# Where a narrow expert's up columns are summed, and which rows a gather fetches: one change to a two-block mixture-of-experts kernel

## The chip, the cores and the metric

The kernel runs on one core of one Trainium2 chip. The metric is the device time of one execution in microseconds (us); three executions of the kernel before are shown, with their median. The profile is a fourth execution, recorded by the hardware profiler.

The engines are called as the profile calls them: PE (TensorE, matrix products), PEld (its weight loads), DVE (VectorE), ACT (ScalarE), POOL (GpSimd), SP (SyncE, which here only issues transfers). Transfers run on 16 DMA engines that all queues share: q1 holds what SP issues, q0 what POOL issues.

## The reference

A transformer block with a short convolution and an expert-choice feed-forward is followed by a second block: an mLSTM and pooling mixer, then a hierarchical mixture of 32 experts. The change touches only the second mixture. Cut to what matters:

```
def hierarchical_moe(h, w_rg, b_rg, w_re, b_re, w_gate, w_up, w_down):
    g_idx = argmax(hf @ w_rg + b_rg)             # one of 4 groups for each of 1024 tokens
    top_val, top_loc = lax.top_k(e_logits, 2)    # 2 of the group's 8 experts
    ...
    def run_block(args):
        a = xb @ w_gate[e]                       # 1024 -> 512
        b = xb @ w_up[e]                         # 1024 -> 512
        return (silu(a) * b) @ w_down[e]         # 512 -> 1024
    out = out * slot_gate[:, None]
    y = zeros((n_tok, dm)).at[slot_tok].add(out)
```

There are 1024 tokens with 2 experts each, 2048 assignments in all. Each expert's three weight matrices are 2 MB each in float32, and all of them are loaded once.

## The kernel before

**Slots.** The 32 experts are put into 32 slots, in an order that depends on how many tokens chose them. A slot has a fixed number of places: 256 (two blocks of 128) in slots 5, 10, 15 and 20 (`PAIRS_AT`), 128 in slots 0 to 2 and in nine more, 64 in slots 26 to 31 (`HALF_AT`), 32 in ten slots (`QUARTER_AT`: 6, 7, 11, 12, 16, 17, 21, 22, 25, 24). Two narrow slots of 32 follow each pair slot, and two more follow slot 23. A place without a token has `src` 0 and `idx` above 8000: `src` names token 0, while `idx` is outside the table, and an indirect transfer skips it (`bounds_check`). The places are 20 x 128 + 6 x 64 + 10 x 32 = 3264.

Counted from the reference's router on the inputs, these are the tokens by slot:

| slots | places each | tokens |
|---|---|---|
| 0, 1, 2 | 128 | 5, 11, 3 |
| 5, 10, 15, 20 | 256 | 158, 169, 213, 162 |
| 3, 4, 8, 9, 13, 14, 18, 19, 23 | 128 | 124, 111, 71, 77, 115, 116, 124, 108, 116 |
| 6, 7, 11, 12, 16, 17, 21, 22, 24, 25 | 32 | 20, 7, 3, 13, 31, 7, 2, 4, 0, 8 |
| 26 to 31 | 64 | 49, 49, 37, 34, 54, 47 |

**Order of work.** `unit_order` writes the program: for slot i, gate (`g`) and up (`u`) products, then the transposes `xT` of slot i+1, then the down product (`d`) of slot i-1, then the transposes `hT` of slot i. So in the program, slot 7's up columns stand ahead of slot 6's down product, and both behind the pair slot 5's down product.

**Weights.** `Loader` issues chunks of 1 MB from SP in exactly that order into 14 buffers (`raw`), with at most four in flight (`N_FLIGHT`). A wide slot's chunk is split in two parts into high and low float32r halves (ACT line 191, DVE line 192, tile `hl`, 5 buffers, `N_SPLIT`), and PE makes three products of them (lines 199 to 201). A narrow slot (32 or 64 places) uses the chunk unsplit (line 556). A buffer is free when its split, or its products, are done.

**Narrow slots of 32 places.** The products leave partial sums in four bands of 32 rows of one PSUM bank. `few_sums` copies two bands to the tile `whole` (ACT line 567; one buffer) and adds the other two to them (DVE line 570): first the gate columns into `hid`, then the up columns into `up`, a piece of an output tile `yo`. ACT applies silu, and DVE line 676 multiplies. The down product's two halves are summed in the same way, into the `yo` that is then scattered.

**Output tiles.** `yo` has two buffers in turn. Each output (DVE line 741 for wide slots, 690/691 for narrow ones) takes one, and POOL scatters it with accumulation into `acc_d` (line 518); the buffer is free when the scatter has landed. Scatters into `acc_d` also wait for each other. The up columns of a narrow slot take a `yo` too, so in the stretch that the prediction reads, the turns are: slot 4's output, slot 6's up, slot 5's two outputs, slot 7's up, slot 6's output, slot 7's output.

**Gathers.** POOL gathers a block's rows of `h_d` (4 KB each) into `xg` (line 512, two buffers) by `src`, at the place where the block before the one before has been transposed. 36 gathers serve the 32 slots.

Of the kernel before, what the change touches and what calls it, by code (L numbers as in the profile page):

```python
# [18 lines left out]
OP = mybir.AluOpType  # L19
# [4 lines left out]
D = 1024  # L24
# [98 lines left out]
def kernel(ctx, tc, a, out):  # L123
    nc = tc.nc
# [7 lines left out]
    def sub_pool(stack, name, bufs=1, side=None):  # L132
        return stack.enter_context(tc.tile_pool(name=name, bufs=bufs, reuse_waits="tile", side=side))
# [8 lines left out]
    def mm_ps(kind="mm"):  # L142
        return banks[kind].tile([P, 2, 512], F32, tag=kind, name=kind)

    def aux_ps(n=512, kind="aux"):
        return banks[kind].tile([P, n], F32, tag=kind, name=kind)
# [33 lines left out]
    acc_d = [dram.tile([T, D], F32, name=f"acc{b}_d") for b in range(2)]  # L180
    h_d = [dram.tile([T, D], F32, name=f"h{b}_d") for b in range(2)]
    mod_d = dram.tile([12, D], F32, name="mod_d")
# [168 lines left out]
    def proj_T(hl, hT, n=P):  # L351

        ps = mm_ps()
        for half in range(2):
            proj_half(ps[:, half], hl, hT, half, n)
        return ps
# [140 lines left out]
    class Experts:  # L497
# [60 lines left out]
        def few_sums(self, ps, m, outs):  # L558

            if m == P // 2:  # L560
                for i, o in enumerate(outs):
                    if o is not None:
                        nc.scalar.copy(o, ps[i * m:(i + 1) * m])
                return
            t = self.tile("whole", [512], 1)
            for at in (P // 2, 0):
                nc.scalar.copy(t[at:at + m], ps[at + m:at + 2 * m])
            for i in (1, 0):
                at = i * (P // 2)
                nc.vector.tensor_tensor(outs[i], ps[at:at + m], t[at:at + m], op=OP.add)  # L570

        def product(self, sT, hl, ps, ks, last):
            for i, k in enumerate(ks):
# [2 lines left out]
    def chunks(e, wg, wu, wd, fdim):  # L576

        b = {}
        for kind, w, kdim, n in (("g", wg, D, fdim), ("u", wu, D, fdim), ("d", wd, fdim, D)):
            m = kdim * n // (P * 2048)  # L580
            b[kind] = [(("x", e, kind, c), w, c, m, n) for c in range(m)]
        return b

    def run_experts(hlp, blocks, route):
# [9 lines left out]
        def ahead(lo=nc.vector):  # L594
            if todo and (todo[0][1] or ld.is_ready(todo[0][0])):
                key, part = todo.popleft()
                if part == 0:
                    raws[key] = ld.take(key)
                raw = raws[key]
                raw = raw[:, part].rearrange("p (h f) -> p h f", h=2) if raw.shape[2] == D else raw[:, part * KP:(part + 1) * KP]  # L600
                hl = hlp.tile([P, 2, KP, 512], F32R, tag="hl", name="hl")
                split(hl, raw, lo)
                if part == N_PARTS - 1:
                    ld.done(key)
                hls.append(hl)
# [19 lines left out]
        ex, late = route(meanwhile)  # L625
        fd = ex.fdim
        subs = deque(s for b in blocks for s in b["subs"])
# [10 lines left out]
        ps, gate_raw = None, None  # L638

        def few(i, kind, c):  # L640

            nonlocal ps, gate_raw
            s = blocks[i]["subs"][0]
            m = s["m"]
            key, _, ci, n_ch, _ = c
            raw = ld.take(key)
            if key[2] == "g":
                gate_raw = key, raw
                if ci == 0:
                    ps = mm_ps()[:, 0]  # L650
                return
            if kind == "u":
                for b in range(4):
                    ex.product_few(s["xT"], (raw[:, b], gate_raw[1][:, b]), ps, ci * 4 + b, 7)
                ld.done(gate_raw[0])
            else:
                if ci == 0:
                    ps = mm_ps()[:, 0]
                for b in range(2):
                    ex.product_few(s["hT"], [raw[:, b, h * 512:(h + 1) * 512] for h in range(2)], ps, ci * 2 + b, 3)  # L660
            ld.done(key)
            for _ in range(N_PARTS):
                if len(hls) < N_SPLIT:
                    ahead()
            if ci < n_ch - 1:
                return
            if kind == "u":
                s["hid"] = hid = ex.tile("hid", [fd], ex.wide)[:m]
                if m == P // 2:
                    nc.scalar.activation(hid, ps[m:], AF.Silu)  # L670
                    nc.vector.tensor_tensor(hid, ps[:m], hid, op=OP.mult)
                else:
                    up = ex.tile("yo", [D], ex.wide)[:m, 0:fd]
                    ex.few_sums(ps, m, (up, hid))
                    nc.scalar.activation(hid, hid, AF.Silu)
                    nc.vector.tensor_tensor(hid, up, hid, op=OP.mult)
                return
            if "keep" in s:
                upper = ex.tile("whole", [512], 1)[:m]
                ex.few_sums(ps, m, (None, upper))  # L680
                s["keep"](ps[:m], s, 0)
                s["keep"](upper, s, 1)
                return
            y = ex.tile("yo", [D], ex.wide)
            if m == P // 2:
                ex.few_sums(ps, m, (None, y[:m, 512:]))
                nc.vector.scalar_tensor_tensor(y[:m, :512], ps[:m], s["gate"][:m], ex.grow[:m, :512], op0=OP.mult, op1=OP.mult)
                nc.vector.scalar_tensor_tensor(y[:m, 512:], y[:m, 512:], s["gate"][:m], ex.grow[:m, 512:], op0=OP.mult, op1=OP.mult)
            else:
                ex.few_sums(ps, m, (y[:m, :512], y[:m, 512:]))  # L690
                nc.vector.scalar_tensor_tensor(y[:m], y[:m], s["gate"][:m], ex.grow[:m], op0=OP.mult, op1=OP.mult)
            ex.scatter(y, s["idx"], m)
            if "after" in s:
                s["after"]()

        for n_unit, (i, kind, c) in enumerate(units):
# [10 lines left out]
            if blocks[i].get("small"):  # L707
                few(i, kind, c)
                continue
            _, _, ci, n_ch, width = c  # L710
            kgs = (fd if kind == "d" else D) // P
            if ci == 0:

                if width == D:
                    ps = [mm_ps() for _ in bl]
                else:
                    two = mm_ps()
                    ps = [two[:, j:j + 1] for j in range(len(bl))]
# [427 lines left out]
    def block2(x_src):  # L1146
# [65 lines left out]
        for h in range(4):  # L1212
            ps = pss[h] if h < 3 else proj_T(ft.next(), hT)
# [9 lines left out]
        with ExitStack() as s3:  # L1223
# [6 lines left out]
            ps = proj_T(wifs, hT, 8)  # L1230
# [3 lines left out]
            for tt in range(NT):  # L1234
                ps = mm_ps()
# [16 lines left out]
        with ExitStack() as s3:  # L1252
# [40 lines left out]
            for slot in range(2 * NT):  # L1293
# [5 lines left out]
                ps = aux_ps(kind="half")  # L1299
# [39 lines left out]
        def ready_tile(tt):  # L1339
# [6 lines left out]
            if tt == NT - 1:  # L1346
# [4 lines left out]
        blocks = [chunks(s, *[w[N_EXP2 - N_FIRST + s] if s < N_FIRST else ("dyn", w, s) for w in ws], 512)  # L1351
                  for s in range(N_EXP2)]
# [18 lines left out]
        with ExitStack() as s3:  # L1371
# [3 lines left out]
            def route2(meanwhile):  # L1375
                sl = s3.enter_context(ExitStack())
                r = route_groups(sub_pool(sl, "rtl2", side="right"), sub_pool(s0, "rt2"), L, meanwhile)
                slot_row[0] = r["row"]
                s0.close()
                for s, b in enumerate(blocks):  # L1380
                    cols = [s] + ([N_EXP2 + PAIRS_AT.index(s)] if s in PAIRS_AT else [])
                    b["subs"] = [dict(src=r["src"][:, c:c + 1], idx=r["idx"][:, c:c + 1], gate=r["gate"][:, c:c + 1]) for c in cols]
                    if b["small"]:
                        b["subs"][0]["m"] = SMALL[s]
                blocks[-1]["subs"][0]["keep"] = keep_rows
                blocks[-2]["subs"][-1]["after"] = load_sums
                ex = Experts(None, sub_pool(s3, "xg2"), h_d[1], acc_d[1], mod_d[11:12, :], 512, 2, wide=2)
                lists.append((r, ex))

                def late():  # L1390
                    yield from r["late"]()
                    yield
                    sl.close()
                    ex.pool = sub_pool(s3, "xp2")
                    ex.row()
                return ex, late()
# [29 lines left out]
            def keep_rows(ps, s, h):  # L1426
# [5 lines left out]
                nc.vector.tensor_tensor(rows[m:, c], y, rows[:m, c].bitcast(F32), op=OP.subtract)  # L1432

            run_experts(hlp, blocks, route2)
            r, ex = lists[0]
            ld.drop_pools()
# [580 lines left out]
```

## Time and profile before

| | |
|---|---|
| median of 3 runs | 2093.81 us (2092.6 to 2098.33) |
| profiled execution, own time | 2095.92 us |
| its span in the trace | 2094.0 us |
| PE, PEld, DVE, ACT, POOL busy | 91%, 71%, 72%, 49%, 16% of the span |
| transfers | 573.56 MB, mean 274 GB/s |

The span is what the trace covers; the time is 1.92 us more. The second mixture fills the span from about 1480 to 2062 us. Busy shares are means over stages with different limits, so the rows below are read by stretch. A DMA share of about 1.02 is what the windows show when the 16 engines are full.

### The profile page before, as it was taken

The page shows a single profiled execution, that of the slowest core. Times are in us where ns is not written, and L with a number is a line of the kernel's source. Part 1 is how long each engine was busy: PE and PEld are TensorE (multiplying, and loading weights), DVE is VectorE, ACT ScalarE, POOL GpSimd, SP SyncE. Part 2 cuts the span into 40 slices and gives each one's busy share as a digit, 9 for nine tenths or more (in the row PEclk, how much of TensorE's full clock was granted, in tenths as well). Part 3 has the DMA queues.
Part 4 walks back from the last instruction along what each step waited for, and adds up shares of the span by engine and source line. Part 5 has one row for each costly group of instructions (what it writes and reads, how often), then busy time and mean ns, then how long its engine had stood idle before and what let it go on. Part 6 is the DMA issues. An engine that isn't in the chain of part 4 may idle for free.

```text
span 2094.0 us, 25405 instructions
## 1 busy us (share of the span) xinstructions
PE 1903.0 (91%) x9192; PEld 1494.4 (71%) x9192; DVE 1502.5 (72%) x1934; ACT 1036.3 (49%) x1454; POOL 332.4 (16%) x300
## 2 busy tenths in 40 slices
PE   4999999949999999999789999898799898898986
PEld 3788888837888888888667787686687576676432
DVE  6699985567999999999744357666896767575414
ACT  4311123216787878787654244332575546464313
POOL 1045430032010110000100000101411211111210
PEclk7999999969999999999989999999899999999998
DMA  9467746288999999999422001426798989999998
GB/s 322 139 231 261 255 160 223 111 295 310 388 384 403 386 402 388 401 381 373 111 97 80 16 31 36 163 111 248 312 387 293 401 325 382 350 391 338 369 386 317
DMA packets 154108, 573.56 MB, mean 274 GB/s; under 512 B 30311, under 2 KB 53575, under 8 KB 104828
## 3 DMA queue, kind: packets, MB, share of 16 engines
q1 hardware_dynamic: 134812, 511.78, 63.5%
q0 software_dynamic: 18784, 59.46, 9.9%
q8 instruction: 73, 1.20, 0.2%
q10 hardware_dynamic: 384, 0.68, 0.1%
q14 instruction: 55, 0.45, 0.1%
HBM read 534.12 MB, written 42.66 MB: 275 GB/s over the span
## 4 chain that ended last, share of the span: by engine, by line
PE 64%; DMA 13%; issue 11%; DVE 7%; ACT 2%; POOL 2%; DVEq 0%; POOLq 0%; SPq 0%; ACTq 0%
PE mm L201 17%; PE mm L199 17%; PE mm L200 17%; DMA raw<-in_w_expert_up_dram 4%; DMA acc_d<-yo,idx 4%; DMA raw<-in_w_expert_down_dram 2%; PE aux L533 2%; PE half L201 1%; PE half L199 1%; PE half L200 1%; PE aux L417 1%; PE aux L1595 1%; POOL acc_d L518 1%; DVE hl L192 1%; POOL xg L512 1%
## 5 line engine op out<-in xcount | busy, mean ns | idle before, releaser
L192 DVE TENSOR_TENSOR hl<-raw,hl 128x1024 fp32r<-128x1024 f32 x601 | 718.2, 1232 | 141.1 <-ACT hl L191 123.1
L191 ACT CAST hl<-raw 128x1024 fp32r<-128x1024 f32 x612 | 634.9, 1054 | 266.6 <-PE mm L201 233.9
L199 PE MATMUL mm<-hl,xT 128*128 128x512 f32 x832 | 331.1, 398 | 0.2 <-ACT xT L195 0.2
L200 PE MATMUL mm<-hl,xT 128*128 128x512 f32 x832 | 327.7, 394 | 0.0
L201 PE MATMUL mm<-hl,xT 128*128 128x512 f32 x832 | 327.7, 394 | 0.0
L199 PE MATMUL mm<-hT,hl 128*128 128x512 f32 x448 | 179.3, 400 | 8.2 <-ACT hT L879 5.9
L199 PEld LDWEIGHTS mm<-hl,xT 128*128 128x128 f32 x832 | 159.1, 191 | 33.2 <-ACT xT L195 0.7
L201 PEld LDWEIGHTS mm<-hl,xT 128*128 128x128 f32 x832 | 158.3, 190 | 34.1 <-issue 0.4
L200 PEld LDWEIGHTS mm<-hl,xT 128*128 128x128 f32 x832 | 158.7, 191 | 32.3
L200 PE MATMUL mm<-hT,hl 128*128 128x512 f32 x448 | 177.0, 395 | 0.2 <-DVE hT L880 0.2
L201 PE MATMUL mm<-hT,hl 128*128 128x512 f32 x448 | 176.6, 394 | 0.0
L199 PE MATMUL mm<-hl,hT 128*128 128x512 f32 x416 | 164.9, 396 | 0.2 <-ACT hT L195 0.2
L201 PE MATMUL mm<-hl,hT 128*128 128x512 f32 x416 | 162.6, 391 | 1.0 <-DVE hT L196 1.0
L200 PE MATMUL mm<-hl,hT 128*128 128x512 f32 x416 | 162.2, 390 | 0.0
L199 PEld LDWEIGHTS mm<-hT,hl 128*128 128x128 f32 x448 | 85.5, 191 | 26.7 <-ACT hT L879 6.4
L556 PE MATMUL mm<-raw,xT 128*32 128x512 f32 (+1 forms) x512 | 85.8, 621 | 16.3 <-DMA raw<-in_w_expert_up_dram 16.3
L301 DVE SCALAR_TENSOR_TENSOR adacc<-adaw,ccol,adacc 128x512 f32<-128x512 f32 x142 | 100.0, 771 | 0.0
L200 PEld LDWEIGHTS mm<-hT,hl 128*128 128x128 f32 x448 | 85.4, 191 | 18.9 <-DVE hT L880 1.4
L518 POOL DMA_INDIRECT acc_d<-yo,idx x35 | 54.0, 1543 | 280.3 <-DVE yo L741 123.9
L201 PEld LDWEIGHTS mm<-hT,hl 128*128 128x128 f32 x448 | 85.3, 190 | 18.1
L201 PEld LDWEIGHTS mm<-hl,hT 128*128 128x128 f32 x416 | 78.1, 188 | 17.9 <-DVE hT L196 1.4
L199 PEld LDWEIGHTS mm<-hl,hT 128*128 128x128 f32 x416 | 78.4, 188 | 16.1 <-ACT hT L195 0.4
(485 smaller groups left out, 2971.7 us busy)
## 6 DMA issues: line engine op xcount, KB each, us to landing
raw<-in_moe_w_gate_dram SPq DMA_DIRECT2D x64, 1024.0 KB
raw<-in_moe_w_up_dram SPq DMA_DIRECT2D x64, 1024.0 KB
raw<-in_moe_w_down_dram SPq DMA_DIRECT2D x64, 1024.0 KB
raw<-in_w_expert_gate_dram SPq DMA_DIRECT2D x64, 1024.0 KB
raw<-in_w_expert_down_dram SPq DMA_DIRECT2D x63, 1024.0 KB
raw<-in_w_expert_up_dram SPq DMA_DIRECT2D x62, 1024.0 KB
adaw<-in_ada_w_dram SPq DMA_DIRECT2D x47, 1024.0 KB
raw<-in_sc_w_in_dram SPq DMA_DIRECT2D x9, 1024.0 KB
```

Source lines behind the costliest of these rows:

```text
L191: nc.scalar.copy(hl[:, 0], raw)
L192: lo.tensor_tensor(hl[:, 1], raw, hl[:, 0].bitcast(F32), op=OP.subtract)
L199: nc.tensor.matmul(o, s_hi, m_hi, start=start, stop=False)
L200: nc.tensor.matmul(o, s_hi, m_lo, start=False, stop=False)
L201: nc.tensor.matmul(o, s_lo, m_hi, start=False, stop=stop)
L301: nc.vector.scalar_tensor_tensor(acc[kk % 2], w[:, k], c, add, op0=OP.mult, op1=OP.add)
L417: nc.tensor.matmul(o, xT[:, k], rsc[:, k], start=k == 0, stop=k == KC - 1)
L512: nc.gpsimd.indirect_dma_start(out=x[:m], out_offset=None, in_=self.src, in_offset=bass.IndirectOffsetOnAxis(ap=idx[:m], axis=0), bounds_c ...
L518: nc.gpsimd.indirect_dma_start(out=self.acc, out_offset=bass.IndirectOffsetOnAxis(ap=idx[:m], axis=0), in_=y[:m], in_offset=None, compute_ ...
L533: nc.tensor.transpose(ps[:, i * P:(i + 1) * P], self.block(x, k, tag), ident)
L556: nc.tensor.matmul(ps[at:at + m], sT[:, k], w, start=k < split, stop=k > last - split)
L1595: nc.tensor.matmul(ps[:, h * P:(h + 1) * P], a_, b_, start=True, stop=True)
```

## The change

Two edits, both in the second mixture.

`few_sums` may now be given `None` for an output, and then sums into the rows of `whole` that hold the copied band, and returns them. A slot of 32 places uses that for its up columns, which no longer take a turn of `yo`.

The gathers of all blocks but the first two use `idx` instead of `src`, so a place without a token is skipped and its row of `xg` keeps what was there. The first two fill both buffers of `xg` with finite rows (`ex_n_x`, 2, is the number of these buffers). A skipped row's result is never scattered.

```
                 at = i * (P // 2)
-                nc.vector.tensor_tensor(outs[i], ps[at:at + m], t[at:at + m], op=OP.add)
+                nc.vector.tensor_tensor(t[at:at + m] if outs[i] is None else outs[i], ps[at:at + m], t[at:at + m], op=OP.add)
+            return t[:m]
...
-                    up = ex.tile("yo", [D], ex.wide)[:m, 0:fd]
-                    ex.few_sums(ps, m, (up, hid))
+                    up = ex.few_sums(ps, m, (None, hid))
                     nc.scalar.activation(hid, hid, AF.Silu)
                     nc.vector.tensor_tensor(hid, up, hid, op=OP.mult)
...
                 r = route_groups(sub_pool(sl, "rtl2", side="right"), sub_pool(s0, "rt2"), L, meanwhile)
                 slot_row[0] = r["row"]
+                ex_n_x = 2
                 s0.close()
...
+                for sub in [sub for b in blocks for sub in b["subs"]][ex_n_x:]:
+                    sub["src"] = sub["idx"]
                 blocks[-1]["subs"][0]["keep"] = keep_rows
                 blocks[-2]["subs"][-1]["after"] = load_sums
-                ex = Experts(None, sub_pool(s3, "xg2"), h_d[1], acc_d[1], mod_d[11:12, :], 512, 2, wide=2)
+                ex = Experts(None, sub_pool(s3, "xg2"), h_d[1], acc_d[1], mod_d[11:12, :], 512, ex_n_x, wide=2)
```

No engine gets or loses an instruction, and none changes its place; the targets and the waits change. On DVE, around slots 5 to 7 of the kernel before (the two L741 are slot 5's outputs, the first two L570 slot 7's gate and up columns, the next two slot 6's down columns; a wait on DMASW is one on a transfer that POOL issued, here a scatter):

```order
L741 SCALAR_TENSOR_TENSOR yo<-mm,gate_11080,grow 128x1024 [waits DMASW4_49,PE_49]
L741 SCALAR_TENSOR_TENSOR yo<-mm,gate_11080,grow 128x1024 [waits DVE_49,PE_49]
L192 TENSOR_TENSOR hl<-raw,hl 128x1024 [waits DMAHW3_49,Activation_49]
L570 TENSOR_TENSOR hid<-mm,whole 32x512 [waits PE_49,Activation_49]
L570 TENSOR_TENSOR yo<-mm,whole 32x512 [waits DMASW6_49,DVE_49]
L676 TENSOR_TENSOR hid<-yo,hid 32x512 [waits DVE_49,Activation_49]
L196 TENSOR_TENSOR xT<-aux,xT 128x512 [waits Activation_49] x2
L570 TENSOR_TENSOR yo<-mm,whole 32x512 [waits DVE_49,PE_49,Activation_49]
L570 TENSOR_TENSOR yo<-mm,whole 32x512
L691 SCALAR_TENSOR_TENSOR yo<-yo,gate_11080,grow 32x1024 [waits DVE_49]
L192 TENSOR_TENSOR hl<-raw,hl 128x1024 [waits Activation_49]
```

The up columns wait there for the scatter of semaphore 6, ahead of slot 8's `xT`. The same place on DVE in the changed kernel:

```order
L741 SCALAR_TENSOR_TENSOR yo<-mm,gate_11080,grow 128x1024 [waits DMASW2_49,PE_49]
L741 SCALAR_TENSOR_TENSOR yo<-mm,gate_11080,grow 128x1024 [waits DMASW4_49,PE_49]
L192 TENSOR_TENSOR hl<-raw,hl 128x1024 [waits DMAHW3_49,Activation_49]
L570 TENSOR_TENSOR hid<-mm,whole 32x512 [waits PE_49,Activation_49]
L570 TENSOR_TENSOR whole<-mm,whole 32x512 [waits DVE_49]
L676 TENSOR_TENSOR hid<-whole,hid 32x512 [waits DVE_49,Activation_49]
L196 TENSOR_TENSOR xT<-aux,xT 128x512 [waits Activation_49] x2
L570 TENSOR_TENSOR yo<-mm,whole 32x512 [waits DMASW6_49,PE_49,Activation_49]
L570 TENSOR_TENSOR yo<-mm,whole 32x512
L691 SCALAR_TENSOR_TENSOR yo<-yo,gate_11080,grow 32x1024 [waits DVE_49]
L192 TENSOR_TENSOR hl<-raw,hl 128x1024 [waits Activation_49]
```

The wait for semaphore 6 has moved three rows down, behind slot 8's `xT`, to slot 6's down columns. The four further pairs of narrow slots change alike. On POOL, as the difference of the two programs, at the third gather (`src` and `idx` are the index tables):

```order
 L92 DMA raw<-in_w_expert_down_dram 128x2048
 L192 TENSOR_TENSOR hl<-raw,hl 128x1024 x2
-L512 DMA xg<-h_d,src_11051 128x1024
+L512 DMA xg<-h_d,idx_11053 128x1024
 L504 DMA grow<-mod_d 128x1024
```

Only the index table of the gather differs; its place does not.

## Rows read from the trace of the kernel before

**Rows 1.** Windows: us; busy PE, PEld, DVE, ACT, POOL; PEclk; DMA share; GB/s
```profile
1640.00:1737.00 97.00, 89.20 (x457) 67.68 (x456) 66.64 (x69) 52.71 (x66) 16.32 (x12) 0.96 0.94 359
1737.00:1834.00 97.00, 88.35 (x457) 67.02 (x456) 66.53 (x68) 52.72 (x66) 15.31 (x12) 0.96 0.98 367
1834.00:1931.00 97.00, 89.88 (x459) 68.13 (x458) 67.11 (x70) 52.71 (x66) 15.34 (x12) 0.96 0.97 363
1931.00:2057.00 126.00, 108.91 (x542) 49.00 (x540) 33.61 (x40) 27.89 (x46) 18.51 (x15) 0.93 1.02 381
```

**Rows 2.** Windows of 10 us, same columns
```profile
1690.00:1700.00 10.00, 10.00 (x48) 8.19 (x47) 5.25 (x6) 3.93 (x5) 0.81 (x1) 1.00 0.53 197
1500.00:1510.00 10.00, 8.63 (x44) 7.20 (x43) 8.34 (x9) 7.03 (x9) 1.03 (x1) 1.00 1.02 418
1630.00:1640.00 10.00, 2.09 (x8) 1.74 (x9) 4.03 (x7) 1.73 (x4) 2.62 (x2) 0.67 1.02 390
```

**Rows 3.** SP's queue waits, 1490 to 2094: total us, times, longest
```profile
SPq L92 <- DVE hl L192: 164.9, 66, 6.0
```

**Rows 4.** Waits of the engines, 1490 to 2094, same columns
```profile
PE aux L541 <- DVE xT L196: 28.1, 4, 8.4
DVE yo L570 <- DMA acc_d<-yo,idx: 27.5, 5, 6.9
```

**Rows 5.** Timeline of DVE: start, us, operation, [idle before]
```profile
1627.87 0.68 DVE L570 TENSOR_TENSOR hid<-mm,whole 32x512 f32<-32x512 f32 x1 [2.30 <-ACT whole L567]
1635.44 0.68 DVE L570 TENSOR_TENSOR yo<-mm,whole 32x512 f32<-32x512 f32 x1 [6.88 <-DMA acc_d<-yo,idx]
...
1637.18 1.27 DVE L196 TENSOR_TENSOR xT<-aux,xT 128x512 fp32r<-128x512 f32 x2
1638.48 1.38 DVE L570 TENSOR_TENSOR yo<-mm,whole 32x512 f32<-32x512 f32 x2
1639.90 1.27 DVE L691 SCALAR_TENSOR_TENSOR yo<-yo,gate,grow 32x1024 f32<-32x1024 f32 x1
```

**Rows 6.** Timeline of ACT, the same stretch
```profile
1629.24 1.07 ACT L195 CAST xT<-aux 128x512 fp32r<-128x512 f32 x2
1641.48 1.04 ACT L191 CAST hl<-raw 128x1024 fp32r<-128x1024 f32 x1 [2.59 <-PE mm L201]
```

**Rows 7.** Timeline of PE, the same stretch
```profile
1637.91 0.68 PE L541 MATMUL aux<-ident,hid 32*128 32x32 f32 x4 [8.36 <-DVE xT L196]
1638.52 0.79 PE L199 MATMUL mm<-hl,xT 128*128 128x512 f32 x1
...
1641.24 0.63 PE L199 MATMUL mm<-hl,xT 128*128 128x512 f32 x1
1641.67 0.63 PE L200 MATMUL mm<-hl,xT 128*128 128x512 f32 x1
...
1644.44 0.39 PE L199 MATMUL mm<-hl,xT 128*128 128x512 f32 x1
1644.67 0.39 PE L200 MATMUL mm<-hl,xT 128*128 128x512 f32 x1
```

**Rows 8.** Chain that ended last, pieces: start, us, what
```profile
1623.53 11.82 DMA acc_d<-yo,idx
...
1636.11 9.67 DMA acc_d<-yo,idx
...
2046.75 10.98 DMA raw<-in_w_expert_down_dram
```

**Rows 9.** Queue q0 in 1602.5:1604.5 (gather of slot 8, 128): packets, MB, share
```profile
q0 software_dynamic: 144, 0.52, 65.5%
```

**Rows 10.** Queue q0 in 1628:1634.5 (scatter, 128)
```profile
q0 software_dynamic: 143, 0.52, 40.6%
```

**Rows 11.** Queue q0 in 1671.5:1673.5 (gather of slot 11, 32 places)
```profile
q0 software_dynamic: 45, 0.13, 21.9%
```

**Rows 12.** Queue q0 in 1748.5:1750 (scatter of slot 11)
```profile
q0 software_dynamic: 33, 0.01, 5.2%
```

## Prediction

> **What bounds the kernel now.** I read the windows first, because the change lies in one stage, the second mixture (1480 to 2062 us), and shares over the whole span mix it with others. From 1640 to 1931 us there are three equal cycles of 97 us. Each holds one pair slot, two narrow slots and two wide ones, 30 chunks of weights. PE is busy for 88 to 90 us of each, and the DMA engines at 0.94, 0.98 and 0.97 [rows 1]. From 1931 to 2057 us, where the half slots come, the DMA share is 1.02 [rows 1], which is what full looks like, and the chain that ended last is a string of weight loads up to the last one [rows 8]. So the end of the stage is set by transfers, and what decides the total is how much work the 16 engines have and how long they sit idle before the last chunk.
>
> Why are they ever idle? The 10 us around 1690 show it: PE busy all the time, DMA share 0.53 [rows 2]. That is the pair slot, where PE needs longest for a chunk; all 14 buffers are full, and SP waits for a split to free one (164.9 us in all) [rows 3]. There PE holds the transfers up, and time that PE loses earlier in the cycle comes back here as idle DMA time.
>
> PE does lose time: 28.1 us in four waits for DVE's `xT` [rows 4]. The timeline shows one. DVE sums slot 7's gate columns at 1627.87 us, then stands 6.88 us at the up columns, since these want the `yo` that slot 5's first output still occupies; its scatter takes 11.82 us from issue to landing [rows 5, 8]. Behind it wait slot 8's `xT`, and behind these PE, idle for 8.36 us [rows 5, 7]. The granted clock is then 0.67 in the mean of these 10 us [rows 2], and the next products come 0.43 us apart instead of 0.23 [rows 7].
>
> **The change part by part, the sums.** DVE does the same additions at the same place. The wait for the scatter moves from slot 7's up columns to slot 6's down columns, three rows further, behind slot 8's `xT`. It isn't removed: it can still last until about 1635.4 us. What is gained is what PE can do meanwhile.
>
> Step by step for this place. The up sum starts where the gate sum ends, 1628.55, and takes 0.68; the product with silu takes about as long, to 1629.95. ACT has the high halves of `xT` ready between 1629.8 and 1630.3 [rows 6]. The first low half takes about 0.68, so PE's transposes start at about 1630.7 instead of 1637.91, 7.2 us earlier [rows 5, 7]; PE's idle time falls from 8.36 to 1.15 us. Its products follow 0.61 later [rows 7], at 1631.3. Five split parts lie ready: ACT could cast a sixth only at 1641.48, when PE had given a buffer back [rows 6]. A part is six products, so at 0.227 us each they last 6.8 us, to 1638.1. DVE comes free from the scatter's landing at 1635.4, plus 1.38 for slot 6's sums, 1.27 for its output [rows 5] and 1.2 for the split, at 1639.3: PE waits 1.2 us. Before, the sixth part's turn came at 1638.52 plus 12 products at 0.43 and 18 at 0.227, or 1647.7 [rows 7]. So PE gains 8.4 us here. If its clock drops anyhow, the five parts last 2.4 us longer, which hides DVE's lateness, and the gain is 7.2.
>
> There are four such places [rows 4]: 28.1 less 4 x 1.15 is 23.5 us that PE starts earlier; with the clock kept, another 2.4 at most for each. PE's side could move by 23 to 31 us.
>
> The transfers cannot follow that far. Against a full 1.02, the cycles' shares leave (0.08 + 0.04 + 0.05) x 97 = 16.5 us of idle [rows 1]; the stretch from 1931 on leaves none.
>
> The second edit makes the transfers' work smaller. The trace shows what a skipped place costs, at the scatters, which already use `idx`: slot 11 has 32 places and 3 tokens; its gather moves 0.13 MB [rows 11], its scatter 0.01 MB, with 33 packets of which all but three are tiny [rows 12]. A gather of 128 full rows has 65.5% of 2.0 us, 1.31 us of all engines or 10.2 ns a row [rows 9]; one of 32 rows 0.44 us or 13.7 ns a row [rows 11]. (A scatter's row costs twice as much, 40.6% of 6.5 us for 128 [rows 10], and stays.) Of 3264 places 1216 are empty; slots 0 and 1 keep their 240, so 976 rows go. 338 of these are in slots 2 to 8, the last of them gathered at 1604 us [rows 9], while PE and full buffers still rule: they buy nothing. After that 638 go, 336 from gathers of 128 and 302 from narrow ones: 3.4 + 4.1 = 7.6 us, or 6.5 at the lower price throughout; I take 7. POOL still issues as many gathers. Bounds for the price of a skipped row: nothing, as at the scatters, or as much as a full row, if the reading is wrong; I take nothing, since it is the same instruction with the same table.
>
> Now both sides together. In the first cycle the transfers' idle time of 7.8 us, and some 1.8 saved by 160 rows, stand against PE's 7.2 to 8.4, so up to 2 us of idle stays. In the second, 3.9 + 1.0 against 5 to 8, and in the third, 4.9 + 2.1 against 6 to 9: none stays, and PE eats into the stock of full buffers, some ten chunks, without emptying it. So the transfers gain 16.5 + 7 - 2 = 21.5 us, and the four places of PE, with 23 to 31, do not bind. The end behind the last chunk (from 2057.7) stays. I take 21.
>
> The profiled time, 2095.92, is 2.1 us above the median, so it goes to 2075 and the median of 2093.81 to 2073, 1.0% less. A measurement here can tell about 0.3%, 6.3 us, from no change.
>
> **A rule against it.** The Trainium skill, DMA: Bandwidth & Descriptors, section Where 436 GB/s comes from, puts transfers between HBM and SBUF under a limit of about 358 GB/s for a core. By that the cycles, at 359 to 367 GB/s, would have nothing to regain. This case's trace doesn't agree: one 10 us window moves 418 GB/s [rows 2]. By the page's rule the change would be worth 7 us, by the rows 21.
>
> **Rivals.**
> 1. *Half the stall comes back.* The wait now stands ahead of the next splits, and slot 7's down columns need the `yo` of slot 5's second output, whose scatter lands 9.67 us after 1636.11, at 1645.8 [rows 8]; with PE 8 us earlier DVE wants it less than 2 us later. If PE keeps only a third to two thirds of its gain, the total is 8 to 17 us: 2077 to 2086.
> 2. *The transfers have no slack.* The windows' dips would then be bursts evened out, and only the 7 us of rows come off: 2087. SP's waits for a free buffer [rows 3] and the 418 GB/s speak against it.
> 3. *The wait only moves.* If PE stood still until DVE passes slot 6's sums, say because the five parts weren't ready, only the tail's 138 rows (24 in slot 25, 114 in the half slots) would count, at 13.7 ns: 1.9 us, 2092. The cast that waited for PE speaks against it [rows 6].
> 4. *More.* If transfers run at their best rate whenever buffers are free, PE's side binds: 25 to 31 us, 2063 to 2069.
> 5. *Slower.* The loads now never pause, so scatters queue behind more of them. From the landing DVE needs 3.9 us to PE's next part; PE is worse off than before once that landing comes after 1647.7 - 3.9 = 1643.8, that is 20.3 us after issue instead of 11.8. At 24 us four places lose 3.7 each: 15 less the tail's 2, 2107. Landings of 10 to 12 us in a stretch that was already full [rows 2, 8] speak against it.
>
> **How the numbers follow.** My forecast, 18 to 25 us off, gets 0.50; rival 1 0.24; rival 2 0.05; rival 3 0.09; rival 4 0.06; rival 5 0.06. The likeliest is 2073, its own range 2069 to 2076. With rivals 1, 2 and most of 4, 2064 to 2088 holds some 0.84. Faster by over 0.3% (below 2087.5): the forecast, rivals 1 and 4, and three fifths of 2, 0.83. Within 0.3%: the rest of 2 and rival 3, 0.11. Slower 0.06.
>
> **What would show it.** In the profile after: no wait of DVE for a scatter at the up columns; a wait of 3 to 6 us at slot 6's down columns and its like; PE's idle time at these places near 1 us, and the clock near 1.00 there; the dips of the DMA share in the pair slots after the first nearly gone; queue q0 smaller by about 4.0 MB (976 x 4096); the dip in slot 5, ahead of these places, unchanged; the stretch behind the last chunk unchanged. It would be wrong if the dips stay although PE no longer waits, or if DVE's new wait grows.

## The result, and the profile after

The changed kernel takes 2075.78 us in the median (2073.99 to 2078.27, 4 runs) against 2094.79 us (2092.6 to 2098.33, 4 runs) beside it: a ratio of 0.9905, with a 95% interval of 0.9893 to 0.9917. That is 19 us faster; 2073 was forecast. The profiled execution took 2075.67 us with a span of 2073.7, 20.3 us less than the span before.

**The place that was worked out.** This is the timeline of DVE in the changed kernel, at the stretch of [rows 5].

```profile
1628.05 0.69 DVE L570 TENSOR_TENSOR hid<-mm,whole 32x512 f32<-32x512 f32 x1 [2.25 <-ACT whole L567]
1628.76 0.68 DVE L570 TENSOR_TENSOR whole<-mm,whole 32x512 f32<-32x512 f32 x1
1629.55 0.68 DVE L676 TENSOR_TENSOR hid<-whole,hid 32x512 f32<-32x512 f32 x1
1630.16 1.27 DVE L196 TENSOR_TENSOR xT<-aux,xT 128x512 fp32r<-128x512 f32 x2
1634.96 1.38 DVE L570 TENSOR_TENSOR yo<-mm,whole 32x512 f32<-32x512 f32 x2 [3.54 <-DMA acc_d<-yo,idx]
1636.38 1.27 DVE L691 SCALAR_TENSOR_TENSOR yo<-yo,gate,grow 32x1024 f32<-32x1024 f32 x1
1637.58 8.02 DVE L192 TENSOR_TENSOR hl<-raw,hl 128x1024 fp32r<-128x1024 f32 x7
...
1648.55 1.38 DVE L570 TENSOR_TENSOR yo<-mm,whole 32x512 f32<-32x512 f32 x2
```

The up columns (second line) start right behind the gate columns. The wait for the scatter is there still, but behind slot 8's `xT` and for 3.54 us. The last line, slot 7's down columns, waits for nothing. And PE's timeline, to set beside [rows 7]:

```profile
1630.88 0.67 PE L541 MATMUL aux<-ident,hid 32*128 32x32 f32 x4 [1.12 <-DVE xT L196]
1631.48 0.50 PE L199 MATMUL mm<-hl,xT 128*128 128x512 f32 x1
...
1638.42 0.39 PE L199 MATMUL mm<-hl,xT 128*128 128x512 f32 x1
1638.84 0.50 PE L200 MATMUL mm<-hl,xT 128*128 128x512 f32 x1
1639.17 0.39 PE L201 MATMUL mm<-hl,xT 128*128 128x512 f32 x1
```

The sixth part's first product, before:

```profile
1647.84 0.39 PE L199 MATMUL mm<-hl,xT 128*128 128x512 f32 x1
```

And the 10 us of [rows 2] that had a granted clock of 0.67, in the changed kernel:

```profile
1630.00:1640.00 10.00, 9.09 (x40) 7.29 (x41) 6.41 (x9) 7.56 (x11) 4.08 (x2) 1.00 1.03 392
```

PE is idle for 1.12 us instead of 8.36, the products stay 0.23 us apart, and the granted clock is 1.00, the upper of its two levels (2.4 GHz). PE takes five split parts in a row. The sixth begins at 1638.42 with the product that reads the high half (line 199), and its second product, which reads the low half, comes after a pause of 0.2 us, at 1638.84.

**The stage.** Waits of the engines after (us in all, times, longest), to set beside [rows 4]:

```profile
DVE yo L570 <- DMA acc_d<-yo,idx: 12.2, 4, 3.5
PE aux L541 <- DVE xT L196: 4.5, 4, 1.1
```

SP's queue, to set beside [rows 3]:

```profile
SPq L92 <- DVE hl L192: 113.4, 45, 6.0
```

SP waits 51 us less for a split to free a buffer. Windows of the changed kernel, three stretches of 92 us and what follows (columns as in [rows 1]):

```profile
1640.00:1732.00 92.00, 88.29 (x464) 67.03 (x463) 67.98 (x70) 53.77 (x67) 28.72 (x13) 1.00 1.00 379
1732.00:1824.00 92.00, 88.74 (x464) 67.08 (x463) 67.24 (x70) 53.92 (x68) 28.41 (x13) 1.00 1.01 383
1824.00:1916.00 92.00, 88.30 (x469) 66.91 (x472) 68.05 (x71) 52.88 (x67) 24.56 (x13) 1.00 1.01 388
1916.00:2040.00 124.00, 101.20 (x502) 41.26 (x498) 25.86 (x34) 21.07 (x40) 18.93 (x15) 0.93 0.99 372
```

The clock is 1.00 instead of 0.96, and the DMA share is at its full 1.00 to 1.01. The last row includes 10 us in which the transfers run out (0.77 from 2030 to 2040). A stretch of 92 us is a little longer than a cycle of the engines. Measured from the output of slot 6 to those of slots 11, 16 and 21 (DVE line 691, at 1639.90, 1736.97, 1834.19 and 1930.76 us before and 1636.38, 1726.60, 1817.57 and 1907.47 after), the sums over three such windows are, before and after:

```profile
sum 290.86, PE 267.29 PEld 202.69 DVE 200.14 ACT 158.14 POOL 46.97; mean PE 89.10 PEld 67.56 DVE 66.71 ACT 52.71 POOL 15.66
sum 271.09, PE 260.38 PEld 196.73 DVE 198.62 ACT 157.60 POOL 80.92; mean PE 86.79 PEld 65.58 DVE 66.21 ACT 52.53 POOL 26.97
```

So a cycle of the engines is 90.4 us instead of 97.0, and PE is busy for 86.8 us of it instead of 89.1. Two single windows of the transfers, the dip that nearly went ([rows 2] had 0.53) and the one ahead of these places, in slot 5, that stayed (0.49 before):

```profile
1590.00:1600.00 10.00, 10.00 (x49) 8.17 (x47) 5.73 (x6) 3.48 (x4) 0.00 (x0) 1.00 0.52 193
1690.00:1700.00 10.00, 10.00 (x65) 7.28 (x68) 8.30 (x9) 6.51 (x8) 1.69 (x2) 1.00 0.90 329
```

The queues of the whole span on the page of after (packets, MB, share):

```profile
q0 software_dynamic: 18784, 55.46, 9.4%
```

Before, q0 had the same 18784 packets and 59.46 MB: 4.00 MB less, which is 976 x 4096 bytes. A skipped row is still a packet, a tiny one.

### The profile page after: what moved, and what is told of

It reads as the page before. It is cut to its first block, busy times and chain, and to the rows that moved or that the text cites. A ratio compares the mean times of both kernels' runs of the same rounds, so it can differ in the third digit from the quotient of the medians.

```text
span 2073.7 us, 25402 instructions
## 1 busy us (share of the span) xinstructions
PE 1895.3 (91%) x9192; PEld 1487.6 (72%) x9192; DVE 1500.4 (72%) x1934; ACT 1036.7 (50%) x1454; POOL 369.9 (18%) x300
## 3 DMA queue, kind: packets, MB, share of 16 engines
q0 software_dynamic: 18784, 55.46, 9.4%
## 4 chain that ended last, share of the span: by engine, by line
PE 76%; DMA 10%; DVE 9%; ACT 2%; issue 2%; POOL 0%; SPq 0%; DVEq 0%; ACTq 0%
PE mm L199 21%; PE mm L201 20%; PE mm L200 20%; DMA raw<-in_w_expert_up_dram 5%; DMA raw<-in_w_expert_down_dram 3%; DVE hl L192 2%; PE aux L533 2%; PE half L201 1%; PE half L200 1%; PE half L199 1%; PE aux L417 1%; PE mm L556 1%; PE aux L1599 1%; DVE adacc L301 1%; DMA raw<-in_w_expert_gate_dram 1%
## 5 line engine op out<-in xcount | busy, mean ns | idle before, releaser
L201 PEld LDWEIGHTS mm<-hl,xT 128*128 128x128 f32 x832 | 156.6, 188 | 33.4 <-issue 0.4
L199 PEld LDWEIGHTS mm<-hl,xT 128*128 128x128 f32 x832 | 157.0, 189 | 32.5 <-issue 0.4
L200 PEld LDWEIGHTS mm<-hl,xT 128*128 128x128 f32 x832 | 156.7, 188 | 32.6 <-DVE hl L192 0.9
L518 POOL DMA_INDIRECT acc_d<-yo,idx x35 | 64.3, 1836 | 259.1 <-DVE yo L741 118.2
L512 POOL DMA_INDIRECT xg<-h_d,idx x34 | 61.4, 1806 | 167.8 <-PE aux L541 112.6
L201 PEld LDWEIGHTS mm<-hl,hT 128*128 128x128 f32 x416 | 78.1, 188 | 17.9 <-DVE hT L196 1.4
```

Source lines behind the costliest of these rows:

```text
L199: nc.tensor.matmul(o, s_hi, m_hi, start=start, stop=False)
L200: nc.tensor.matmul(o, s_hi, m_lo, start=False, stop=False)
L201: nc.tensor.matmul(o, s_lo, m_hi, start=False, stop=stop)
L512: nc.gpsimd.indirect_dma_start(out=x[:m], out_offset=None, in_=self.src, in_offset=bass.IndirectOffsetOnAxis(ap=idx[:m], axis=0), bounds_c ...
L518: nc.gpsimd.indirect_dma_start(out=self.acc, out_offset=bass.IndirectOffsetOnAxis(ap=idx[:m], axis=0), in_=y[:m], in_offset=None, compute_ ...
```

## The experiments

For each run the time, and from its profile three numbers that tell the stage apart from what lies ahead of it: the stretch from the first gather of the second mixture to the issue of the last chunk of up weights, and the transfers' idle time from 1620 to 1940 us (the sum of 1.02 less the share over 32 windows of 10 us). Each profile is one execution; an empty cell was not compared.

| kernel | median us | ratio to before, 95% interval | first gather to last up chunk, us | idle, us |
|---|---|---|---|---|
| before | 2094.79 to 2096.48 | | 1479.0 to 2041.76: 562.8 | 17.3 |
| changed | 2075.78 | 0.9905 (0.9893 to 0.9917) | 1478.0 to 2020.51: 542.5 | 3.3 |
| first edit alone | 2083.92 | 0.9938 (0.9925 to 0.9952) | 1481.5 to 2030.91: 549.4 | 1.3 |
| second edit alone | 2093.6 | 0.9986 (0.9977 to 0.9995) | 1480.3 to 2037.18: 556.9 | 20.1 |
| rows from slot 9 on | 2075.0 | 0.9900 (0.9885 to 0.9915) | 1479.8 to 2020.87: 541.1 | 3.0 |
| 32 rows a gather | 2070.7 | 0.9877 (0.9862 to 0.9892) | 1480.3 to 2017.38: 537.1 | 5.5 |
| PE work, 141 us | 2179.0 | 1.0392 (1.0375 to 1.0409) | | |
| PE work, 38 us | 2088.69 | 0.9971 (0.9960 to 0.9983) | 1477.7 to 2032.58: 554.9 | 15.6 |
| five loads in flight | 2075.66 | 0.9901 (0.9885 to 0.9918) | | 5.1 |
| one narrow slot early | 2070.02 | 0.9872 (0.9856 to 0.9889) | 1480.3 to 2015.91: 535.6 | 3.0 |
| two narrow slots early | 2071.24 | 0.9871 (0.9854 to 0.9888) | 1480.4 to 2018.89: 538.5 | 9.3 |
| splits with one input and a sum | 2100.79 (one run) | | 1491.1 to 2046.41: 555.3 | |
| splits with one input | 2087.04 (one run) | | 1493.0 to 2034.34: 541.4 | |

**The first edit alone.** To the kernel before:

```
-                nc.vector.tensor_tensor(outs[i], ps[at:at + m], t[at:at + m], op=OP.add)
+                nc.vector.tensor_tensor(t[at:at + m] if outs[i] is None else outs[i], ps[at:at + m], t[at:at + m], op=OP.add)
+            return t[:m]
...
-                    up = ex.tile("yo", [D], ex.wide)[:m, 0:fd]
-                    ex.few_sums(ps, m, (up, hid))
+                    up = ex.few_sums(ps, m, (None, hid))
```

> The kernel before with the first edit alone: up columns of the 32-place slots summed in whole, all gathers by src as before. My theory (PE's stalls held the transfers up, and these had 16.5 us of idle time to regain in the three cycles): the idle time less some 1 to 2 us, 14 to 16 us off the time before, 2079 to 2081 us; PE's waits for xT fall to some 5 us in all, the dips of the DMA share in the later pair slots go, and the windows of the cycles show a share of about 1.02. Rival 2 (transfers have no slack, only the skipped rows count): no change, 2092 to 2095. Rival 3 (the wait only moves): PE's waits for xT stay near 28 us, no change.

Measured: 12.2 us off, with no row left out, somewhat less than the 14 to 16 expected. PE's waits for `xT` fell to 4.5 us in all. Rivals 2 and 3 are out. The windows show the transfers full through the cycles, which is the point of my theory; 16.0 us of idle went, but only 13.4 of it is seen up to the last up chunk (from 1490 to 1620 and from 1940 to 2040 us idle time rose by 1.3).

```profile
1640.00:1734.50 94.50, 90.20 (x471) 68.28 (x470) 70.16 (x73) 55.37 (x70) 30.90 (x14) 1.00 1.01 389
1734.50:1829.00 94.50, 90.97 (x477) 69.11 (x476) 69.81 (x73) 55.22 (x70) 30.90 (x13) 1.00 1.02 385
1829.00:1923.50 94.50, 89.36 (x476) 66.49 (x474) 67.63 (x70) 53.35 (x68) 24.93 (x14) 1.00 1.02 387
```

The sum over the engines' three cycles, from slot 6's output (1640.46 us) to slot 21's (1912.10):

```profile
sum 271.64, PE 260.11 PEld 196.56 DVE 198.69 ACT 157.31 POOL 80.83; mean PE 86.70 PEld 65.52 DVE 66.23 ACT 52.44 POOL 26.94
```

The engines go through the cycles as fast as in the changed kernel (271.09 us), and yet the stretch up to the last up chunk is 6.9 us longer. So with the first edit made it is the transfers that set the total, and the second edit acts on them.

**The second edit alone.** To the kernel before:

```
+                for sub in [sub for b in blocks for sub in b["subs"]][2:]:
+                    sub["src"] = sub["idx"]
```

> The kernel before with the second edit alone: gathers after the first two by idx, up columns in yo as before. My theory: in the three cycles PE's stalls set the pace, so the 500 rows skipped there only make the dips of the DMA share deeper; the tail's 138 rows count, 1.9 us, so 2092 to 2094. Rival 2 (no slack in the transfers): the 638 rows after slot 8 count in full, 6.5 to 7.6 us, 2087 to 2088. If a skipped row cost as much as a full one: no change, and q0 as large as before.

Measured: 2.5 us between the medians, 2.9 by the ratio (1.0 to 4.8 by its interval), which agrees with my theory and lies below the 6.5 to 7.6 of rival 2. The dips are where they were, and the idle time grew by 2.8 us: the rows made the transfers' work smaller, and PE made them wait longer. Three stretches of 96 us, and the sum over the engines' three cycles (1639.89 to 1929.35 us):

```profile
1640.00:1736.00 96.00, 87.69 (x456) 66.59 (x455) 66.16 (x68) 52.74 (x66) 15.58 (x12) 0.96 0.95 359
1736.00:1832.00 96.00, 87.92 (x451) 66.41 (x450) 64.75 (x66) 52.15 (x65) 14.08 (x11) 0.96 0.95 356
1832.00:1928.00 96.00, 88.92 (x461) 67.55 (x461) 67.80 (x71) 53.06 (x67) 16.98 (x14) 0.96 0.95 361
sum 289.46, PE 265.99 PEld 201.71 DVE 200.11 ACT 158.22 POOL 47.41; mean PE 88.66 PEld 67.24 DVE 66.70 ACT 52.74 POOL 15.80
```

The share fell in two of them, the GB/s did not rise, and the engines' cycles stay near 97 us. But this profile is less clear than the times. If the 500 rows in the cycles had bought nothing, idle time would have grown by 5.1 us (at 10.2 ns a row) and not by 2.8, and up to the last up chunk this execution is 5.9 us shorter than the one before. With the first edit made, the same rows are worth 8.1 us between the medians (2083.92 to 2075.78), 6.9 by the ratios and 6.9 by the stretches. By the ratios the two edits together give 19.9 us against 15.9 for the sum of each alone, with intervals of 2 to 3 us either way; by the stretches 20.3 against 19.3. That they help each other is therefore not shown.

**Which rows count.** The changed kernel with

```
-                for sub in [sub for b in blocks for sub in b["subs"]][ex_n_x:]:
+                for sub in [sub for b in blocks for sub in b["subs"]][10:]:
```

> The changed kernel, but the gathers of slots 2 to 8 go by src again, so 338 of the 976 rows come back. My theory: these lie where PE and full buffers rule, so the time is that of the changed kernel, 2074 to 2077. Rival (any row saved is time saved, at 10.2 to 13.7 ns): 3.4 to 4.6 us slower, 2079 to 2081.

Measured: the time of the changed kernel. The 338 rows of slots 2 to 8 buy nothing; all of the second edit's worth lies in the 638 behind them.

**Fewer rows still.** The changed kernel, in `gather`, with `self.rows` 32 for the second mixture:

```
+            m = min(m, self.rows)
```

> The changed kernel, but each gather of the second mixture fetches at most the first 32 rows of its block; what lies behind them in xg is left from earlier, so the outputs of these tokens are not the reference's. It takes about 1170 rows away, some 890 of them from slot 9 on (some 8.3 us in the three cycles and 0.8 us in the half slots, at 10.2 ns a row). It tells what binds after the change. My theory (transfers bind, PE has some 3 to 4 us of idle time left in each cycle): 6 to 9 us off, 2067 to 2070. Rival (PE's side binds again after the change): only the half slots' rows, 2074 to 2075.

Measured: 5.1 us off, a little less than my range, and more than the rival allows. The transfers do bind still, but PE is close: idle time rose from 3.3 to 5.5 us.

**PE's side, twice.** The changed kernel, in `few`, behind the gate and up products:

```
+                if m == P // 4:
+                    more = aux_ps()
+                    for b in range(4):
+                        for w in (raw, gate_raw[1]):
+                            nc.tensor.matmul(more[:m], s["xT"][:, ci * 4 + b], w[:, b], start=True, stop=True)
```

> The changed kernel with PE work added: behind the gate and up products of each slot of 32 places, 16 further products of 512 columns whose result nobody reads, some 3.6 us a slot at 0.227 us each, 7.3 us a cycle, 29 us over the first four pairs of such slots. It asks from the other side how far PE is from binding after the change. My theory (transfers bind, PE has 3.5 us idle in a cycle, and the stock of full buffers takes up some more): the first 3.5 us of each cycle cost nothing, the rest does once the stock is used up, so 6 to 14 us over the changed kernel, 2081 to 2089. If transfers alone bind with much room on PE: at most 2 us over. If PE binds throughout: 25 to 29 us over, 2101 to 2104.

Measured: 103 us over the changed kernel, outside of all three. The sizing was wrong, so the run decides between none of them: the groups of PE show 320 instructions and 140.7 us added, where I had put 36 us.

```profile
L660 PE MATMUL aux<-raw,xT 128*32 128x512 f32 x320 | 140.7, 592 | 0.1
```

So the run says only that 37 of 141 us found room. The second one has one pair of products a chunk instead of four:

```
-                    for b in range(4):
-                        for w in (raw, gate_raw[1]):
-                            nc.tensor.matmul(more[:m], s["xT"][:, ci * 4 + b], w[:, b], start=True, stop=True)
+                    for w in (raw, gate_raw[1]):
+                        nc.tensor.matmul(more[:m], s["xT"][:, ci * 4], w[:, 0], start=True, stop=True)
```

> As in the run with PE work added, but sized by what that run showed: a product of float32 rows is two instructions on PE, and one of them took 0.44 us where all go into one band, so the 16 products a slot were 14 us and not 3.6. Here four products a slot, eight instructions, 3.5 us; 7.0 us a cycle, 28 us over the first four pairs of narrow slots, 35 us in all. My theory (PE has 3.7 us idle in each cycle of 92 us, some 23 us behind them, and a stock of full buffers): 5 to 14 us over the changed kernel, 2080 to 2090. If transfers alone bind with much room on PE: at most 2 us over. If PE binds throughout: 25 us or more over, 2100 and up.

Measured: 12.9 us over the changed kernel for 37.7 us of PE work, inside my range. One cycle of the engines shows what binds then:

```profile
1639.16:1734.32 95.16, 93.85 (x474) 67.63 (x473) 66.45 (x69) 52.73 (x67) 15.75 (x12) 1.00 0.95 361
```

PE is busy for 93.9 of 95.2 us, and the share falls to 0.95 (0.99 and 0.96 in the next two cycles). The changed kernel is near both limits: the transfers are full, and PE has 3.3 to 3.7 us idle in each of its cycles of 90.4 us.

**Five loads in flight.** `N_FLIGHT` 4 to 5 in the changed kernel.

> The changed kernel with five weight loads in flight instead of four, in the whole program. If the transfers are full once nothing holds them up (a DMA share of 1.01 to 1.02 in the cycles), a deeper queue gives nothing there: 2073 to 2078. Rival (the engines run dry between two loads, and a deeper queue fills the gaps): 2 to 5 us faster in the second mixture.

Measured: no change.

**The idle time ahead of the cycles.** `QUARTER_AT` of the changed kernel is `(6,7,11,12,16,17,21,22,25,3)` in the one, `(6,7,11,12,16,17,21,22,4,3)` in the other.

> The changed kernel with one slot of 32 places moved: slot 24 becomes a slot of 128 places and slot 3 one of 32. In the changed kernel the transfers lose some 13.9 us between 1490 and 1620 us (the sum of 1.02 less the share over the 10 us windows), while PE works without a pause through slots 0 to 5. A narrow slot takes some 11 us less of PE than a wide one. My theory (idle transfer time ahead of the last chunk is what decides): PE comes to slot 5 some 11 us earlier, 8 to 11 us of that idle time go, and PE's longer work behind slot 23 lies where it has 23 us to spare: 2064 to 2068. Rival (PE behind slot 20 is then too late, and the same idle time comes up there): no change, 2073 to 2077.

> The changed kernel with both slots of 32 places behind slot 23 moved ahead: slots 24 and 25 have 128 places, slots 3 and 4 have 32. My theory: all of the 13.9 us of idle transfer time before 1620 goes, but PE has 22 us more to do behind slot 23, where its spare time is 23 us, so part of it may come back there: 2061 to 2068. Rival (PE is too late behind slot 20): 2070 or more, no better than with one moved.

Measured: 5.8 and 4.5 us off the changed kernel. The first beats both kernels, its interval lies below that of the changed one, but it gave less than expected: from 1570 to 1620 us idle time fell from 9.9 to 6.9 us only, not by the 8 to 11 expected. With two moved it fell to 2.0 us, and came up again one pair slot later: 9.3 us instead of 3.3 from 1620 on. These two windows of that run show it:

```profile
1670.00:1680.00 10.00, 10.00 (x46) 8.29 (x45) 4.22 (x4) 5.01 (x6) 0.00 (x0) 1.00 0.76 289
1680.00:1690.00 10.00, 10.00 (x56) 7.97 (x59) 7.87 (x8) 5.59 (x8) 1.06 (x1) 1.00 0.60 210
```

I had looked for a loss behind slot 20; it is in slot 10. Why one move regains so little ahead of slot 5 stays open.

**What holds POOL up.** In the changed kernel POOL is busy for 369.9 us instead of some 332. Its timeline shows where, one of three such gathers in the stage; before, the gather of that place took 1.06 us.

```profile
1637.48 9.06 POOL L512 DMA_INDIRECT xg<-h_d,idx  x1 [0.30 <-PE mm L201]
```

The seven splits on DVE end at 1645.60, the gather at 1646.54. The next two runs replace these splits, which read two tiles of SBUF, by an operation that reads one and leaves the low halves at zero. The first is this edit, the second the same without `accum_out`:

```
-                split(hl, raw, lo)
+                if n == N_EXP2 and lo is nc.vector:
+                    nc.scalar.copy(hl[:, 0], raw)
+                    nc.vector.tensor_scalar(hl[:, 1], raw, 0.0, 0.0, op0=OP.mult, op1=OP.add, accum_out=junk1)
+                else:
+                    split(hl, raw, lo)
```

> The changed kernel with another operation on DVE for the low halves of the second mixture's splits: zero times the chunk, with the sum written beside it, so that DVE reads one tile of SBUF and not two, and the low halves are zero (the products lose their correction; outputs are less exact). In the changed kernel a gather that POOL starts while DVE makes seven low halves in a row shows 9.06 us instead of 1.0 (and so in each run with the first edit). If it is DVE's two inputs from SBUF that hold POOL up: the longest gather falls to some 1 to 2 us, the longest scatter from 5.2 to 2.4 us, POOL's busy time to that of the kernel before, and the time hardly moves (2066 to 2078), since nobody waited for POOL there. If any run of DVE does it: the gather stays at 6 us or more.

> The same with the sum left out (zero times the chunk, one tile read, low halves zero). If only DVE's two inputs from SBUF hold POOL up, gathers are at 1 to 2 us as in the run with the sum; if this form runs in a faster mode of DVE that takes the same way into SBUF, its instructions are shorter than 1.07 us and a gather still waits for the end of their run. The time: 2066 to 2078.

The one with the sum, DVE and then POOL (the DVE run goes on to 1664.7):

```profile
1655.29 1.20 DVE L606 TENSOR_SCALAR_CACHE_REDUCE hl<-raw 128x1024 fp32r<-128x1024 f32 x1
1656.43 0.07 DVE L606 DVE_READ_ACCUMULATOR hl<-raw 128x1 f32 x1
```

```profile
1655.19 1.11 POOL L512 DMA_INDIRECT xg<-h_d,idx  x1 [0.30 <-issue]
```

The one without it, in the same order:

```profile
1651.09 2.48 DVE L606 TENSOR_SCALAR hl<-raw 128x1024 fp32r<-128x1024 f32 x4
```

```profile
1651.08 2.63 POOL L512 DMA_INDIRECT xg<-h_d,idx  x1 [0.30 <-issue]
```

Measured: with one tile read and the sum, the gather takes 1.11 us though DVE works all along, and the longest scatter of the stage 1.63 us; POOL is down to 332.0 us. Without the sum the splits take 0.62 to 0.69 us instead of 1.15 to 1.2, and the gather ends 0.14 us behind their run of four. So it is what DVE's operation reads and in which form, not that DVE is busy. The stall isn't in each run with the first edit: with 141 us of PE work the longest gather of the stage took 1.87 us. The times of the two runs without two-input splits, 2100.79 and 2087.04 us of one run each, miss what was expected: in both the second mixture's first gather comes 12 to 14 us later than before (1491.1 and 1493.0), for a reason that I did not look for. In the run with the sum the stretch up to the last up chunk is also 12.8 us longer than in the changed kernel, in the one without it 1.1 us shorter. So these times do not tell what POOL's stall costs.

## Why the prediction was right

**The place.** Transposes were worked out for 1630.7 us and came at 1630.88, products 1631.3 and 1631.48, PE's idle time 1.15 and 1.12. The clock stayed. PE's pause at the sixth part is 0.2 us instead of 1.2: the landing came 0.4 us sooner (1634.96 instead of 1635.4), the five parts ended 0.3 us later (1638.42 instead of 1638.1), and the sixth part's first product, 0.2 us, does not need the low half. That product moved from 1647.84 to 1638.42: 9.4 us, 8.4 forecast.

**The four places.** PE's waits for `xT`: 4 x 1.15 = 4.6 us forecast, 4.5 measured. DVE's moved wait: 3 to 6 us each forecast; 2.4 to 3.5 measured, two of the four below 3. PE's side was to move by 23 to 31 us; DVE's outputs of slots 21 and 22 came 23.3 and 27.7 us sooner (1930.76 to 1907.47 and 1948.24 to 1920.49). (The sum there is off: 23.5 plus four times 2.4 is 33.1, not 31. The forecast does not rest on it.) The clock's part was put at 2.4 us at most; PE's busy time in a cycle fell by 2.3.

**The transfers.** They bind, as forecast: PE's side gained 23 us and more, the whole 20.3. Their idle time was put at 16.5 us, with 2 left; by the finer windows it was 17.3, and 3.3 are left, so 14.0 were regained. The rows were put at 7 us; at 10.2 ns the 638 are worth 6.5, and 14.0 + 6.5 is 20.5 against 20.3 measured between the first gather and the last up chunk. The sum was 21.5, taken as 21. That the first edit alone gives 12.2 us where I expected 14 to 16 shows the term of the idle time some 2 to 3 us too large; the second edit on top of it gives 7 to 8. So the close fit of the sum is partly luck, and by the medians, 19 us, the result lies at the slow end of the range of 2069 to 2076.

**Left alone.** The dip in slot 5 stayed, the 338 rows ahead of slot 9 bought nothing (idle time from 1490 to 1620 us rose from 11.5 to 13.9), and from the last up chunk to the end there were 52.2 us before and 53.2 after.

**The rule that spoke against it.** By the Trainium skill, DMA: Bandwidth & Descriptors, section Where 436 GB/s comes from, a core's traffic with HBM ends at about 358 GB/s. By that the change would have been worth the rows alone, 7 us. The cycles now move 379 to 388 GB/s, and the first edit alone, which takes no byte away, gave 12.2 us. The measurement decides against it here.

**The rivals.** Rival 1 fell because seven splits stand between slot 6's and slot 7's down columns: DVE wants the second `yo` at 1648.55 us and finds it free. Rivals 2 and 3 fell with the first edit alone. Rival 4 was near: PE's side did gain 23 to 28 us, but the transfers were full, and 38 us more on PE cost 13. For rival 5 the scatters would have had to land 20.3 us after issue; the one of 1623.75 had landed by 1634.96, after 11.2 us.

## What to carry to other kernels

Ask of each stage which side would bind if the other's stalls were gone, and add up that side's idle time: it caps what a removed stall can give, however long the stall. Less work for the transfers counts where they set the pace: the 338 rows fetched while PE and full buffers ruled bought nothing, and the 638 behind them some 7 us. Whether these would have been worth less without the first edit, as the times say (2.5 to 2.9 us) and the profiles do not (5.9), stays open. A wait for a buffer needn't be removed, if it can be moved behind the work that another engine is waiting for.

## What the runs showed of the hardware

**POOL held up by DVE's reads.** Seven subtractions in a row on DVE, each of two SBUF tiles, made a 1.06 us indirect gather 9.06 us, three times in the stage (9.06, 9.06 and 9.07). The Trainium skill, SBUF — State Buffer, section Who interferes with whom, says that an operation of DVE with two SBUF inputs contends with what GpSimd reads there, that `tensor_scalar` can take the shared ports too but not in the form that writes its accumulator out, and infers that writing descriptors isn't stalled by `tensor_tensor`. The three runs agree with the first two (9.06, 2.63 and 1.11 us). Against the last, an indirect gather as a whole does stall; which part of it does is not shown. Among the waits of the changed kernel none is for such a gather.

**Four bands at once.** In the first run with more PE work, products of one shape go into four bands of a bank, then all into one band:

```profile
1638.34 1.92 PE L556 MATMUL mm<-raw,xT 128*32 128x512 f32 x16
1640.08 6.60 PE L660 MATMUL aux<-raw,xT 128*32 128x512 f32 x15
```

Sixteen over four bands take 1.92 us, 0.12 each; fifteen in one band 6.60, 0.44 each, 3.7 times as much. I had sized them by neither row.
